# The last three stores of a decoder layer: a 256-column piece by ScalarE, GpSimd and a second store queue, and the stores of the block before it in halves

## The chip, the cores and the metric

The kernel runs on one core of a Trainium2 chip. The metric is the device time of one execution in microseconds, as the median of several runs. A core has TensorE (PE, matmuls), VectorE (DVE), ScalarE (ACT), GpSimd (POOL) and SyncE (SP), which here issues transfers. The core's 16 DMA engines move the data of all queues.

## The reference, cut to what matters

The layer takes x of 512 tokens by 1024 channels through two attention branches and a gated MLP. Only its last line bears on the change:

```python
ffn_out = (jax.nn.silu(h_gate) * h_val) @ w_down
x = _layer_norm(DEEPNORM_ALPHA * x + (1.0 + gt2) * ffn_out, ln2_g, ln2_b)
```

The layer norm takes each token's mean mu and variance over its 1024 channels and gives (x - mu) * rs * g + b, with rs = 1 / sqrt(var + 1e-5). All data is 32-bit float.

## The kernel before, in words

**Tiling.** The 512 tokens are four blocks of 128 rows (one row to a partition), each held as two tiles of 512 columns, `r[i][0]` and `r[i][1]`. The down projection is a chain of matmuls that ends with blocks 2 and 3. Blocks 0 and 1 are finished earlier, in `first_rows` (line 1298). Blocks 2 and 3 are finished by the last loop of `layer_kernel` (line 1345). For `i == 0` (block 2) columns 512 to 1023 are one piece of 512. For `i == 1` (block 3) they are two pieces of 256, whose matmuls run one after the other, so that only the last 256 columns come after the last matmul.

**The end of a block.** `tail` (line 1239) is called with the block number, 2 or 3, as its own `i`. It calls `ln_stats` (line 899), in which VectorE and ScalarE make mu and rs from the statistics in `st`. Line 1245 then has VectorE take (v - mu) * g of each piece, and line 1249 has VectorE take v * rs + b. After each piece's line 1249, line 1250 stores it from `nc.sync`, that is, from SP's queue. Block 2 has two pieces of 512 columns (256 KB each). Block 3 has three, called A, B and C here: A is columns 0 to 511 (256 KB), B is columns 512 to 767 and C is columns 768 to 1023 (128 KB each). B is the "middle" piece of the change.

**What sets the order.** SP runs in the order of the program, since `manual_schedule` at line 55 names that engine; a transfer waits there for the data, and what is behind it waits too. The other engines' instructions are ordered by a scheduler within the limits of their dependences: VectorE runs the small steps of `ln_stats` between the pieces of line 1245. The dependences are kept by part of a tile. ScalarE has nothing after the square root of line 903 in block 3, and GpSimd has nothing after the stores of line 1308.

Of the kernel before, what the change touches and what calls it, by code (L numbers as in the profile page):

```python
# [11 lines left out]
AF = mybir.ActivationFunctionType  # L12
ALU = mybir.AluOpType
# [11 lines left out]
H = T // 2  # L25
# [26 lines left out]
def layer_kernel(ctx: ExitStack, tc: tile.TileContext, out, xT, x, c8, wa0, wa1, bcol, w1, wct, wv, bf,  # L52
# [3 lines left out]
    V, S, G, PE = nc.vector, nc.scalar, nc.gpsimd, nc.tensor  # L56
# [63 lines left out]
    s = V.tensor_tensor(sel, s3, ident[:, 64:72], ALU.add)  # L120
    def top_half(ap):
        return ap.bitcast(BF16).rearrange("p (c t) -> p c t", t=2)[:, :, 1]

    ctop = top_half(crow)
    with tc.issue_after(s.ins):
        s = V.tensor_tensor(crow[32:40], c8s, top_half(c8s), ALU.subtract)
# [772 lines left out]
    def ln_stats(st):  # L899
        mv = cons.tile([P, 8], F32, name=nm("mv"), tag="mv", bufs=2)  # L900
        V.bn_aggr(mv[:, 0:2], st)
        v, s, y, t = mv[:, 2:3], mv[:, 3:4], mv[:, 4:5], mv[:, 5:6]
        S.activation(s, mv[:, 1:2], AF.Sqrt, bias=epsc)
        V.tensor_scalar_add(v, mv[:, 1:2], EPS)
        V.reciprocal(y, s)
        V.scalar_tensor_tensor(t, y, y, v, ALU.mult, ALU.mult)
        V.scalar_tensor_tensor(y, t, -3.0, y, ALU.add, ALU.mult)
        return mv[:, 0:1], y
# [16 lines left out]
    lnr = []  # L925
# [245 lines left out]
    for n in range(2 * FT):  # L1171
# [34 lines left out]
        if n % 2 == 1:  # L1206
            g, v = hc
# [31 lines left out]
    def tail(i, st, pieces, eng, src):  # L1239
        tb = slice(i * P, (i + 1) * P)  # L1240
        mu, rs = ln_stats(st[:, 0 : len(pieces), :])
        for (e, c0, c1), ps in zip(pieces, src):
            c = slice(e * 512 + c0, e * 512 + c1)
            v = r[i][e][:, c0:c1]
            V.scalar_tensor_tensor(v, v if ps is None else ps, mu, lnr[0][:, c], ALU.subtract, ALU.mult)
        for e, c0, c1 in pieces:
            c = slice(e * 512 + c0, e * 512 + c1)
            v = r[i][e][:, c0:c1]
            V.scalar_tensor_tensor(v, v, rs, lnr[1][:, c], ALU.mult, ALU.add)
            eng.dma_start(out[tb, c], v)  # L1250

    p1, u2, q1, u3, tm = [[fine(n) for _ in range(2)] for n in ("p1", "u2", "q1", "u3", "tm")]

# [63 lines left out]
    lnr = lnr2  # L1317
# [21 lines left out]
    s = V.tensor_tensor(r[3][1], r[3][1], W1[1], ALU.add)  # L1339
# [5 lines left out]
    for i in range(2):  # L1345
        pieces = [(1, 0, 512)] if i == 0 else [(1, 0, 256), (1, 256, 512)]
        for n, (e, c0, c1) in enumerate(pieces):
            ps = bank()[:, 0 : c1 - c0] if i else W1[0]
            for m in range(2 * n):
                PE.matmul(ps, idr, rest[:, m * 256 : m * 256 + 256], start=m == 0, stop=False)  # L1350
            for q in range(LATE):
                t = ops[FP - LATE + q][3]
                product(ps, t[:, top[i]], t[:, bot[i]], wc[q][0][:, c0:c1], wc[q][1][:, c0:c1], i == 1 and n == 0 and q == 0, q == LATE - 1, i == 0)
            v = r[2 + i][e][:, c0:c1]
            if n == 0:
                V.tensor_tensor(v, v, ps, ALU.add)
            V.bn_stats(sts[i][:, n + 1, :], ps if n else v)
        tail(2 + i, sts[i], [(0, 0, 512)] + pieces, nc.sync, [None, None, ps] if i else [None] * 2)
# [69 lines left out]
```

## Time and profile before

| what | value |
|---|---|
| median of 3 runs | 734.93 us (734.62 to 735.27) |
| the profiled execution, its time | 734.07 us |
| the profiled execution, its span | 732.3 us |
| PE busy in the span | 722.5 us (99%) |
| DVE, ACT, POOL busy | 601.1, 391.7, 88.0 us |

The span runs from the first to the last profiled instruction; 1.8 us of the profiled execution's time lie around it. Times in the rows are microseconds from the start of the span. A view of instructions has their start, their duration and the line of the kernel. A view of stretches has, for each, its length, each engine's busy time, the granted TensorE clock as a share of full speed, the mean busy share of the 16 DMA engines and the GB/s that they moved.

### The profile page before, as it was taken

The page shows a single profiled execution, that of the slowest core. Times are in us where ns is not written, and L with a number is a line of the kernel's source. Part 1 is how long each engine was busy: PE and PEld are TensorE (multiplying, and loading weights), DVE is VectorE, ACT ScalarE, POOL GpSimd, SP SyncE. Part 2 cuts the span into 40 slices and gives each one's busy share as a digit, 9 for nine tenths or more (in the row PEclk, how much of TensorE's full clock was granted, in tenths as well). Part 3 has the DMA queues.
Part 4 walks back from the last instruction along what each step waited for, and adds up shares of the span by engine and source line. Part 5 has one row for each costly group of instructions (what it writes and reads, how often), then busy time and mean ns, then how long its engine had stood idle before and what let it go on. Part 6 is the DMA issues. An engine that isn't in the chain of part 4 may idle for free.

```text
span 732.3 us, 9843 instructions
## 1 busy us (share of the span) xinstructions
PE 722.5 (99%) x3444; PEld 602.5 (82%) x3444; DVE 601.1 (82%) x1041; ACT 391.7 (53%) x684; POOL 88.0 (12%) x142
## 2 busy tenths in 40 slices
PE   8999999999999999999999999999999999999995
PEld 5878888888888888888889888888888888888885
DVE  7978799778898886883687999978887887679996
ACT  5576466686885754442056553454453544347550
POOL 1045224352010000000000001000011010000010
PEclk9999999999999999999999999999999999999998
DMA  9953435323332241632075688587698777657734
GB/s 358 404 207 126 173 116 197 148 88 115 118 116 99 75 171 59 224 128 86 1 259 139 216 248 238 169 252 227 189 359 245 217 238 209 200 164 224 219 91 93
DMA packets 45202, 131.96 MB, mean 180 GB/s; under 512 B 6136, under 2 KB 6656, under 8 KB 45152
## 3 DMA queue, kind: packets, MB, share of 16 engines
q1 hardware_dynamic: 37888, 112.61, 44.6%
q0 software_dynamic: 4224, 10.30, 7.4%
q10 hardware_dynamic: 3040, 8.42, 3.1%
q8 instruction: 27, 0.44, 0.2%
q14 instruction: 23, 0.19, 0.1%
HBM read 118.39 MB, written 12.85 MB: 179 GB/s over the span
## 4 chain that ended last, share of the span: by engine, by line
PE 97%; DVE 1%; DMA 0%; ACT 0%; issue 0%; DVEq 0%
PE ps L152 19%; PE ps L154 19%; PE ps L153 19%; PE ps L1148 5%; PE ps L1149 5%; PE ps L1150 5%; PE ps L369 5%; PE ps L613 3%; PE ps L595 2%; PE ps L521 2%; PE ps L523 2%; PE ps L522 2%; PE ps L939 2%; PE ps L941 2%; PE ps L940 2%; PE ps L547 1%
## 5 line engine op out<-in xcount | busy, mean ns | idle before, releaser
L217 ACT ACTIVATE wh<-raw 128x1024 fp32r<-128x1024 f32 (+1 forms) x105 | 109.0, 1040 | 106.5 <-PE ps L153 43.2
L94 DVE TENSOR_TENSOR wl<-raw,wh 128x1024 fp32r<-128x1024 f32 (+2 forms) x114 | 137.3, 1205 | 32.4 <-ACT wh L217 31.6
L152 PE MATMUL ps<-u2h,wh 128*128 128x512 f32 (+1 forms) x376 | 141.5, 376 | 0.0
L153 PE MATMUL ps<-u2l,wh 128*128 128x512 f32 (+1 forms) x376 | 141.3, 376 | 0.0
L154 PE MATMUL ps<-u2h,wl 128*128 128x512 f32 (+1 forms) x376 | 141.3, 376 | 0.0
L154 PEld LDWEIGHTS ps<-u2h,wl 128*128 128x128 f32 x376 | 70.8, 188 | 12.9
L152 PEld LDWEIGHTS ps<-u2h,wh 128*128 128x128 f32 x376 | 70.8, 188 | 12.7
L153 PEld LDWEIGHTS ps<-u2l,wh 128*128 128x128 f32 x376 | 70.8, 188 | 12.6
L152 PE MATMUL ps<-uh,wh 128*128 128x512 f32 x200 | 79.6, 398 | 0.0
L154 PE MATMUL ps<-uh,wl 128*128 128x512 f32 x200 | 78.2, 391 | 0.0
L153 PE MATMUL ps<-ul,wh 128*128 128x512 f32 x200 | 78.0, 390 | 0.0
L1201 ACT ACTIVATE cv<-ps,cw 128x512 f32<-128x512 f32 x44 | 34.0, 773 | 42.4 <-PE ps L154 36.0
L1202 DVE SCALAR_TENSOR_TENSOR cv<-ps,cw,cv 128x511 f32<-128x511 f32 x44 | 32.8, 746 | 21.6 <-ACT cv L1201 21.5
L154 PEld LDWEIGHTS ps<-uh,wl 128*128 128x128 f32 x200 | 37.6, 188 | 8.4
L153 PEld LDWEIGHTS ps<-ul,wh 128*128 128x128 f32 x200 | 37.7, 188 | 7.4
L152 PEld LDWEIGHTS ps<-uh,wh 128*128 128x128 f32 x200 | 37.6, 188 | 7.3
L240 DVE SCALAR_TENSOR_TENSOR raw<-raw,cbc 128x1024 f32<-128x1024 f32 x32 | 39.6, 1240 | 0.0
L575 POOL TENSOR_TENSOR pt<-pt,om 128x127 f32<-128x127 f32 (+3 forms) x32 | 38.6, 1217 | 1.3 <-DVE om L574 1.3
L181 POOL DMA_DIRECT2D raw<-in_wdp x10 | 8.9, 889 | 243.8 <-DMA raw<-in_wdp 227.7
L1203 DVE SCALAR_TENSOR_TENSOR cv<-ps,cw,cv 128x510 f32<-128x510 f32 x44 | 32.7, 744 | 0.4
L1209 ACT ACTIVATE cv<-cv 128x512 f32<-128x512 f32 x22 | 13.9, 631 | 34.1 <-DVE cv L1203 34.1
L574 DVE TENSOR_TENSOR_SCAN om<-om,dg 128x127 f32<-128x127 f32 (+3 forms) x32 | 28.8, 960 | 3.9 <-ACT om L569 3.9
(245 smaller groups left out, 1551.0 us busy)
## 6 DMA issues: line engine op xcount, KB each, us to landing
raw<-in_wup SPq DMA_DIRECT2D x44, 512.0 KB, 5.0
raw<-in_wa SPq DMA_DIRECT2D x32, 512.0 KB, 3.7
raw<-in_wct SPq DMA_DIRECT2D x25, 512.0 KB, 4.5
raw<-in_wdp SPq DMA_DIRECT2D x20, 512.0 KB, 5.3
wa<-in_wa SPq DMA_DIRECT2D x16, 512.0 KB, 8.7
raw<-in_wdp SPq DMA_DIRECT2D x22, 256.0 KB, 4.9
raw<-t SPq DMA_DIRECT2D x22, 256.0 KB, 4.3
raw<-in_wdp POOLq DMA_DIRECT2D x10, 512.0 KB, 7.7
```

What stands on the lines that cost most here:

```text
L94: state["read"] = V.tensor_tensor(o, i, fl(hi), ALU.subtract)
L152: PE.matmul(ps, wh, ah, start=first, stop=False)
L153: PE.matmul(ps, wh, al, start=False, stop=False)
L154: return PE.matmul(ps, wl, ah, start=False, stop=last)
L217: state["hi"] = S.activation(h[:, 0:cols], r[:, 0:cols], AF.Copy)
L240: state["read"] = V.scalar_tensor_tensor(wt[:, c], wt[:, c], 1.0, cbc[:, c] if by is None else by, ALU.mult, ALU.mult, accum_out=o)
L369: m = PE.matmul(grp[g], w, u, start=j == 0 and n == 0, stop=j == KT - 1 and n == 2)
L575: G.tensor_tensor(pt[b][:, s : e - 1], pt[b][:, s : e - 1], om[:, s + 1 : e], ALU.mult)
L1148: PE.matmul(ps, ah, bh, start=first, stop=False, skip_group_check=onto)
L1149: PE.matmul(ps, ah, bl, start=False, stop=False, skip_group_check=onto)
L1150: return PE.matmul(ps, al, bh, start=False, stop=last, skip_group_check=onto)
L1201: S.activation(t, ps, AF.Identity, bias=cw[:, n, 3:4], scale=cw[:, n, 2:3])
```

## The change

In `tail`, for the one piece whose block has three pieces and that starts at column 512 (piece B of block 3), line 1249 and the store of line 1250 are replaced by three instructions: ScalarE multiplies by rs, GpSimd adds b, and the store is issued from ScalarE's queue. In addition each store of block 2 becomes two stores of 256 columns (`H` is 256), both from SP's queue; A and C of block 3 are stored as before.

```diff
         for e, c0, c1 in pieces:
             c = slice(e * 512 + c0, e * 512 + c1)
             v = r[i][e][:, c0:c1]
+            if len(pieces) == 3 and c0 == 0 and e == 1:
+                S.activation(v, v, AF.Copy, scale=rs)
+                G.tensor_tensor(v, v, lnr[1][:, c], ALU.add)
+                S.dma_start(out[tb, c], v)
+                continue
             V.scalar_tensor_tensor(v, v, rs, lnr[1][:, c], ALU.mult, ALU.add)
-            eng.dma_start(out[tb, c], v)
+            for q in range(2) if i == 2 else [None]:
+                s = slice(0, c1 - c0) if q is None else slice(q * H, q * H + H)
+                eng.dma_start(out[tb, e * 512 + c0 : e * 512 + c1][:, s], v[:, s])
```

## Rows read from the trace of the kernel before

**Rows 1.** The page: span and the chain that ended last, by engine.

```profile
span 732.3 us, 9843 instructions
PE 97%; DVE 1%; DMA 0%; ACT 0%; issue 0%; DVEq 0%
```

**Rows 2.** Timeline of VectorE after the last matmul: start, duration, line, operation.

```profile
727.41 0.15 DVE L907 SCALAR_TENSOR_TENSOR mv<-mv 128x1 f32<-128x1 f32 x1
727.59 0.75 DVE L1249 SCALAR_TENSOR_TENSOR xn<-xn,mv,ln 128x512 f32<-128x512 f32 x1
...
728.26 0.88 DVE L1249 SCALAR_TENSOR_TENSOR xn<-xn,mv,ln 128x256 f32<-128x256 f32 x2
...
728.66 0.48 DVE L1249 SCALAR_TENSOR_TENSOR xn<-xn,mv,ln 128x256 f32<-128x256 f32 x1
```

**Rows 3.** Timeline of SP's queue: block 2's two stores merged, then A, B, C.

```profile
723.81 1.00 SPq L1250 DMA_DIRECT2D out<-xn  x2
...
728.37 0.33 SPq L1250 DMA_DIRECT2D out<-xn  x1
...
728.81 0.37 SPq L1250 DMA_DIRECT2D out<-xn  x1
...
729.28 0.39 SPq L1250 DMA_DIRECT2D out<-xn  x1
```

**Rows 4.** Stretches from block 2's first data to C's last.

```profile
724.60:726.10 1.50, 0.32 (x3) 0.12 (x1) 1.07 (x4) 0.29 (x1) 0.00 (x0) 1.00 0.92 350
726.10:727.60 1.50, 0.00 (x0) 0.00 (x0) 1.47 (x7) 0.00 (x0) 0.00 (x0) 1.00 0.01 5
727.60:729.20 1.60, 0.00 (x0) 0.00 (x0) 1.54 (x3) 0.00 (x0) 0.00 (x0) 0.77 0.00 0
729.20:729.90 0.70, 0.00 (x0) 0.00 (x0) 0.00 (x0) 0.00 (x0) 0.00 (x0) 0.50 0.96 367
729.90:730.30 0.40, 0.00 (x0) 0.00 (x0) 0.00 (x0) 0.00 (x0) 0.00 (x0) 0.50 0.99 336
730.30:730.70 0.40, 0.00 (x0) 0.00 (x0) 0.00 (x0) 0.00 (x0) 0.00 (x0) 0.50 0.92 320
```

**Rows 5.** DMA issues from 728.3 us on: count, KB each, median us to landing.

```profile
out<-xn SPq DMA_DIRECT2D x1, 256.0 KB, 2.0
out<-xn SPq DMA_DIRECT2D x2, 128.0 KB, 2.1
```

**Rows 6.** Line 1424, the program's end: SP's waits, ns min/median/max, first and last start.

```profile
L1424 SPq EVENT_SEMAPHORE  x12: 17/28/28, 729.7 to 732.2; - x12
```

**Rows 7.** ScalarE's groups over the whole span: busy us, mean ns, idle before.

```profile
L91 ACT ACTIVATE wdh<-rl 128x512 fp32r<-128x512 f32 x8 | 4.9, 617 | 0.3 <-DMA rl<-wgt 0.3
...
L91 ACT ACTIVATE hv<-sg 128x256 fp32r<-128x256 f32 x33 | 11.4, 405 | 0.0
```

**Rows 8.** Line 1307, ScalarE's scaling by rs: ns min/median/max, first and last start.

```profile
L1307 ACT ACTIVATE xn<-xn,mv x4: 705/708/727, 708.7 to 712.6; 128x512 f32<-128x512 f32 x4
```

**Rows 9.** Timeline, attention: GpSimd's 255-column product beside VectorE's scan, and later alone.

```profile
55.72 1.81 DVE L574 TENSOR_TENSOR_SCAN om<-om,dg 128x511 f32<-128x511 f32 x1
...
56.45 1.51 POOL L575 TENSOR_TENSOR pt<-pt,om 128x255 f32<-128x255 f32 x1
...
166.32 0.64 POOL L575 TENSOR_TENSOR pt<-pt,om 128x255 f32<-128x255 f32 x1
```

**Rows 10.** Line 1198, two stores to the output from ScalarE's queue: ns each, starts.

```profile
L1198 ACTq DMA_DIRECT2D out<-ln x2: 357/359/361, 535.2 to 536.6; - x2
```

**Rows 11.** DMA issues of ScalarE's queue: count, KB each, median us to landing.

```profile
t<-raw ACTq DMA_DIRECT2D x10, 512.0 KB, 2.7
...
out<-ln ACTq DMA_DIRECT2D x2, 512.0 KB, 5.8
```

**Rows 12.** The stretch in which line 1198 issues.

```profile
534.00:537.00 3.00, 3.00 (x15) 2.48 (x14) 1.08 (x4) 1.46 (x2) 2.08 (x4) 1.00 1.02 417
```

## Prediction, made before the run

> **What bounds the kernel now.** I read the page first, for what share of the span the change can touch at all. Its chain is 97% matmuls [rows 1], and the change touches none of them. It can act only after the last matmul, so I went to VectorE's timeline there: rs of block 3 is ready at 727.41 + 0.15 = 727.56 [rows 2]. From there to the end of the span are 732.3 - 727.56 = 4.74 us, 0.64% of the time. That is all the change has to work on.
>
> The next question is which wait ends last inside those 4.74 us. VectorE works through A, B and C back to back: A 727.59 to 728.34, B from 728.26, C from 728.66 to 729.14 [rows 2]. SP issues each store behind it, at 728.37, 728.81 and 729.28 [rows 3]. Read alone, those two views say that the chain is vector work and issue, and that taking B out of both would bring the end nearer. The table of stretches says otherwise. No data moves until 729.20, which is 0.83 us after A's issue. Then the DMA engines are 0.92 to 0.99 busy without a break until 730.70 [rows 4]. They move A (262,144 bytes) at 367 GB/s, 0.71 us, to 729.91, and B and C (131,072 bytes each) at 336 and 320 GB/s, 0.39 and 0.41 us, to 730.30 and 730.71. C was issued at 729.28, so by the same 0.83 us its data could have started at 730.11. The engines were not free for it until 730.30. **C has 0.19 us of slack**: it waits for transfers ahead of it, not for VectorE or SP. What follows is completion: the stores land 2.0 to 2.1 us after their issue, C at about 731.3 [rows 5], and SP's closing waits run to 732.2 [rows 6].
>
> So three things bound the end: the moment A is issued, 512 KB at some 350 GB/s, and the completion of the last piece. The change alters none of the three.
>
> **The change, part by part.**
>
> *B leaves VectorE.* That removes one line 1249 of 256 columns, 0.40 us of VectorE's path (728.26 to 728.66, start to start [rows 2]). C could then be done 0.40 us earlier, at 728.74, and be issued at 728.81, where B's store was. A stays first and starts at 727.59 as before; its store stays at 728.37.
>
> *B on ScalarE.* Line 1307 is this very operation at 512 columns, also behind a square root on ScalarE: 0.71 us, and no load of a function table stands among its instructions [rows 8], so I add none. Plain copies of 512 and 256 columns differ by 617 - 405 = 212 ns [rows 7], so I take 0.71 - 0.21 = 0.50 us. The handover from VectorE to SP takes 0.03 us (728.34 to 728.37 [rows 2, 3]); with the same to ScalarE it runs from 727.59 to 728.09.
>
> *B on GpSimd.* The nearest row is the 255-column product in attention: 0.64 us by itself, 1.51 us beside a scan on VectorE [rows 9]. With under 0.1 us of handover the add can start at 728.15, while A is still on VectorE until 728.34, with C next. Bounds: it ends at 728.79 if undisturbed and at 729.66 at the longer price. I take a wait for A and then the 0.64: 728.98. It is nearer the lower end because only 0.2 us of A is left when the add starts, against 1.08 us of the scan in the row of 1.51 (56.45 to 57.53). What VectorE loses in return is C: between nothing and the add's 0.64, so C ends between 728.74 and 729.38.
>
> By the Trainium skill, "SBUF — State Buffer", section "Who interferes with whom", a VectorE instruction with two SBUF inputs and a GpSimd one that reads SBUF exclude each other, and the later one waits for all of the other; this speaks against the change. By that rule the add would run from 728.34 to 728.98 and C from there to 729.46, and the data would end within 0.02 us of before. The trace agrees with the rule only in part: the product beside the scan would have ended at 57.53 + 0.64 = 58.17 by it, and ended at 57.96 [rows 9].
>
> *B's store from ScalarE's queue.* It issues at about 729.0 (729.7 at the longer price) and takes 0.36 us on that queue [rows 10]; nothing is behind it there. GpSimd too has nothing behind the add. First data by the same 0.83 us is at 729.83 (730.53). C's data can be ready by 728.81 + 0.83 = 729.64, or by 729.41 + 0.83 = 730.24 if the add holds C to 729.38. In the likely case both halves are there before or close to when A's data is through at 729.91, in one order or the other, and the third piece is needed only at 730.30, that is, issued by 729.47. So both moves cost or gain **nothing**: the cover is A's 0.71 us and one half's 0.39 us on the DMA engines. If that cover were gone, the gain would be the earlier issue of the last store, at most 729.28 - 728.81 = 0.47 us. At the longer price for the add, B's data starts at 730.53 instead of 730.30: 0.23 us later.
>
> *Block 2's stores in halves.* SP issues four instead of two: two behind the first instruction of line 1249, from 723.81, and two behind the second. Before, the two took until 724.81 [rows 3]. Stores of block 3 follow each other at 0.44 to 0.47 us, so the extra pair adds 0.9 us at most and SP is done by 725.8, or 2.6 us before A needs it at 728.37. The halves move at about 330 instead of 350 to 367 GB/s, 0.1 us more for 512 KB, so that the engines finish near 726.3; they then stand idle until 729.20 [rows 4]. Cost zero; cover 2.6 us on SP and 2.9 us on the DMA engines, and 0.9 us if that were gone.
>
> *The closing.* SP has 12 waits of up to 28 ns here [rows 6], and a different last store or a second queue can shift a few. I take -0.1 to +0.1 us.
>
> **Sum.** Against the profiled execution (734.07 us, span 732.3 us): 0 for vector work and issue, 0 for block 2, about -0.1 for a last store that no longer queues behind two others on SP, hence some 734.0 for such an execution. It was 0.86 us under the median of 734.93, so I put the change on the median: 734.8 us.
>
> **The rivals.**
>
> *Issue-bound after all (faster, 0.04).* If the engines' 0.92 to 0.99 busy share hides a wait for C's issue, the last store comes 0.47 us sooner: 734.5. For it: 320 GB/s in the last stretch is below A's 367. Against: no gap of idle engines between 729.20 and 730.70 [rows 4].
>
> *GpSimd and VectorE in each other's way (0.05).* The add at 1.51 us makes B the last piece, +0.23 us: 735.2. For: the 1.51 us of the nearest row [rows 9]. Against: only 0.2 us of A remain when the add is ready.
>
> *ScalarE's queue is slow to deliver (slower, 0.03).* Its two earlier stores to the output took 5.8 us from issue to landing [rows 11], against 2.0 to 2.1 on SP's queue [rows 5]. With B issued at 729.0 and landing 5.8 us later, at 734.8 against 731.3 now, the end comes 3.5 us later: 738.4. It costs something once the landing takes longer than 2.3 us, and can be measured from 3.8 us on. Against: those were 512 KB each, at DMA engines that were full (share 1.02 [rows 12]); ten other stores of 512 KB from that queue landed in 2.7 us [rows 11], of which 512 KB at 350 GB/s are 1.5.
>
> *The change does not reach B.* The condition holds for exactly one piece: three pieces only in block 3, and column 512 only in B. I give it no chance.
>
> **How the numbers follow.** About 0.2%, 1.47 us, is what a measurement of this kernel can tell from no change. On the slow side only the slow queue exceeds it, 0.03, and 0.01 is left for what the rows do not show: 0.04. A gain of 1.47 us would be a third of the 4.74 us; no case here has it, and 0.02 is left for the unseen. The rest, 0.85 for the forecast and 0.09 for the two small rivals, is within: 0.94. The range takes the spread of the three runs (734.62 to 735.27), less 0.47 and 0.1 below, plus 0.23 and 0.1 above: 734.0 to 735.6.
>
> **What would show it.** Right: A issued 0.81 us after rs, the DMA engines full from its first data for 1.5 us without a gap, and some 3.1 us from that first data to the end of the span. ScalarE 0.50 us, GpSimd's add 0.64 to 0.9 us, C's end between 728.74 and 729.38 on this clock. Block 2's four stores done 2.5 us or more before A's. Wrong: idle DMA engines between the three pieces, a landing of B much over 2.1 us, or a span before the last matmul that is not the same to a few tenths.

## The result, and the profile after

The changed kernel takes 737.09 us in the median of 8 runs (736.48 to 737.71), against 734.85 us for the kernel before (8 runs, 734.62 to 735.27). The ratio is 1.0028, with a 95% interval of 1.0020 to 1.0037: it is slower by some 2 us, where the prediction said 734.8 us, at most 735.6, and gave a slowdown one chance in 25.

The span of the profiled execution grew from 732.3 to 734.7 us. Not all of these 2.4 us belong to the change: rs of block 3 is there at 727.73 + 0.15 = 727.88 instead of 727.56, so 0.32 us were lost before the first changed instruction that matters, among matmuls that are the same in both programs. Such differences come and go between executions (in experiment 11, whose program is that of before up to this point, rs is there at 728.50); what stands behind rs is the subject here, and the times below are given from rs.

The stages of the last block come first. The four fences are the timelines of VectorE, ScalarE, GpSimd and SP after the change (start, duration, line, operation); line 1254 is the old 1249, and 1250 to 1252 are the three new instructions.

```profile
727.73 0.15 DVE L907 SCALAR_TENSOR_TENSOR mv<-mv 128x1 f32<-128x1 f32 x1
727.92 1.61 DVE L1254 SCALAR_TENSOR_TENSOR xn<-xn,mv,ln 128x512 f32<-128x512 f32 x2
```

```profile
727.92 0.51 ACT L1250 ACTIVATE xn<-xn,mv 128x256 f32<-128x256 f32 x1 [1.54 <-DVE mv L907]
729.28 0.34 ACTq L1252 DMA_DIRECT2D out<-xn  x1
```

```profile
728.51 0.74 POOL L1251 TENSOR_TENSOR xn<-xn,ln 128x256 f32<-128x256 f32 x1 [13.52 <-ACT xn L1250]
```

```profile
728.70 0.33 SPq L1257 DMA_DIRECT2D out<-xn  x1
...
729.56 0.33 SPq L1257 DMA_DIRECT2D out<-xn  x1
```

Everything here is as forecast. ScalarE needs 0.51 us (0.50 forecast), GpSimd's add ends at 729.25, which is rs + 1.37 (1.42 forecast), and C is ready at 729.53, which is rs + 1.65 (between 1.18 and 1.82 forecast). A is issued 0.82 us after rs, as before. The stretches show the engines full from the first data to the last, over the same 1.5 to 1.6 us as in [rows 4] (columns as there):

```profile
727.10:729.50 2.40, 0.00 (x0) 0.00 (x0) 2.36 (x6) 0.51 (x1) 0.74 (x1) 0.97 0.01 2
729.50:730.20 0.70, 0.00 (x0) 0.00 (x0) 0.03 (x1) 0.00 (x0) 0.00 (x0) 0.50 0.94 357
730.20:730.60 0.40, 0.00 (x0) 0.00 (x0) 0.00 (x0) 0.00 (x0) 0.00 (x0) 0.50 0.96 330
730.60:731.10 0.50, 0.00 (x0) 0.00 (x0) 0.00 (x0) 0.00 (x0) 0.00 (x0) 0.50 0.82 285
731.10:734.70 3.60, 0.00 (x0) 0.00 (x0) 0.00 (x0) 0.00 (x0) 0.00 (x0) 0.50 0.00 0
```

The data of all three stores is out at 731.1. Before, it was out at 730.7, with rs 0.32 us earlier, so that the stores are level within 0.1 us. But then 3.6 us pass to the end of the span, where 1.6 passed before. The loss lies behind the last byte. What happens there is the program's closing, and all of it has one line, 1431 (1424 before). On each engine's own queue (POOLq is GpSimd's, SPq is SP's) it has DRAIN instructions and the semaphores at which all engines meet. The view of that line, in the changed kernel (count, ns min/median/max, first and last start):

```profile
L1431 SPq EVENT_SEMAPHORE  x11: 17/28/28, 729.9 to 734.6; - x11
L1431 POOLq EVENT_SEMAPHORE  x4: 17/17/17, 734.0 to 734.6; - x4
L1431 POOLq DRAIN  x3: 46/98/5447, 728.5 to 734.4; - x3
L1431 SPq DRAIN  x3: 7/7/7, 731.7 to 734.2; - x3
```

And the same view of the kernel before, from which [rows 6] has only SP's waits:

```profile
L1424 POOLq EVENT_SEMAPHORE  x4: 17/17/17, 731.6 to 732.2; - x4
L1424 POOLq DRAIN  x3: 46/98/8165, 713.5 to 732.0; - x3
L1424 SPq DRAIN  x3: 7/7/7, 731.5 to 731.8; - x3
```

SP's own first DRAIN, behind its waits for the stores, stands at 731.7 (731.5 before). GpSimd's first semaphore of the closing stands at 734.0, against 731.6 before. Between them lies GpSimd's longest DRAIN: it starts with the add at 728.5 and lasts 5.447 us, to 733.9. Before, it lasted even longer, 8.165 us, but it started at 713.5 with GpSimd's last store and was over by 721.7, ten microseconds before anyone asked. SP's drains take 7 ns in both kernels, though SP issues transfers too. The other engines show the wait, under a misleading name. SP's waits in the changed kernel:

```profile
SPq L1431 <- PEq L1431: 2.9, 2, 2.4
SPq L1431 <- DMA out<-xn: 1.2, 3, 0.5
```

and in the kernel before:

```profile
SPq L1424 <- DMA out<-xn: 1.2, 3, 0.5
SPq L1424 <- PEq L1424: 0.7, 2, 0.5
```

The wait for the stores is the same 1.2 us. The wait at the meeting of the engines grew from 0.7 to 2.9 us. The view puts it down to PE, whose queue has been idle for long; it is a meeting of all engines, and GpSimd comes last.

### The profile page after: what moved, and what is told of

Read it like the earlier page. It is cut to its first block, busy times and chain, and to the rows that moved or that the text cites. A ratio compares the mean times of both kernels' runs of the same rounds, so it can differ in the third digit from the quotient of the medians.

```text
span 734.7 us, 9844 instructions
## 1 busy us (share of the span) xinstructions
PE 723.1 (98%) x3444; PEld 602.2 (82%) x3444; DVE 600.5 (82%) x1040; ACT 392.2 (53%) x685; POOL 88.6 (12%) x143
## 4 chain that ended last, share of the span: by engine, by line
PE 97%; DVE 1%; DMA 0%; ACT 0%; DVEq 0%; issue 0%
PE ps L152 19%; PE ps L154 19%; PE ps L153 19%; PE ps L1148 5%; PE ps L1150 5%; PE ps L1149 5%; PE ps L369 5%; PE ps L613 3%; PE ps L595 2%; PE ps L521 2%; PE ps L523 2%; PE ps L522 2%; PE ps L939 2%; PE ps L940 2%; PE ps L941 2%; PE ps L547 1%
```

## The experiments

**Theory D**: GpSimd's closing drain outlasts its last instruction by some 4.7 us, and every engine waits for it. **Rival Q**: ScalarE's queue or the halves of block 2 deliver late. **Rival C**: VectorE and GpSimd block each other. Four kernels take these apart.

**1. B's add on VectorE.**

```diff
                 S.activation(v, v, AF.Copy, scale=rs)
-                G.tensor_tensor(v, v, lnr[1][:, c], ALU.add)
+                V.tensor_tensor(v, v, lnr[1][:, c], ALU.add)
                 S.dma_start(out[tb, c], v)
```

> The changed kernel with one word altered: B's add of b runs on VectorE instead of GpSimd; ScalarE's scaling, the store from ScalarE's queue and block 2's halves stay. Theory D (GpSimd's closing drain at the program's end lasts some 4.7 us beyond its last instruction, and every engine waits for it): GpSimd's last work is line 1315's stores at about 715 again, its drain is over by about 722, and the time is that of before within 0.3 us, 734.6 to 735.1, that is 2.0 to 2.4 us under the changed kernel. Rival Q (ScalarE's queue delivers late, or the halves cost): still about 737. Rival C (VectorE and GpSimd block each other): part of it comes back, since B's add returns to VectorE, 735 to 736.

Measured: 734.71 us, 0.9999 of the kernel before (0.9990 to 1.0008). The whole loss goes with the one instruction; ScalarE's scaling, its queue and the halves stay and cost nothing that can be told.

**2. A GpSimd copy of one column, late, in the kernel before.**

```diff
             eng.dma_start(out[tb, c], v)
+        if len(pieces) == 3:
+            G.tensor_copy(const([P, 1], F32, "touch"), v[:, 0:1])
```

> The kernel before, with one GpSimd copy of 128x1 added that reads C's result after VectorE's last instruction and that nothing reads. No other part of the change is in it. Theory D: the copy is done at about 729.3, the drain at about 729.3 + 4.7 = 734.0 instead of being over long before 731.6, and the time is 2.0 to 2.6 us over before, 736.9 to 737.5. Rival Q: no store differs, so 734.9. Rival C: nothing of VectorE runs beside it, so 734.9.

Measured: 736.73 us, 1.0027 (1.0016 to 1.0037). None of the change is in this kernel but a GpSimd instruction of 0.19 us on data that nobody needs, and it costs what the change costs. Its timeline and its closing:

```profile
729.34 0.19 POOL L1252 COPY touch<-xn 128x1 f32<-128x1 f32 x1 [14.54 <-DVE xn L1249]
```

```profile
L1426 POOLq DRAIN  x3: 46/93/4871, 729.3 to 734.7; - x3
```

**3. The same copy, early.**

```diff
             eng.dma_start(out[tb, c], v)
+        if len(pieces) == 2:
+            G.tensor_copy(const([P, 1], F32, "touch"), v[:, 0:1])
```

> The same GpSimd copy of 128x1, but reading block 2's last result, at about 724.5. Theory D: the drain is over at about 724.6 + 4.7 = 729.3, before the last store has landed at 731.3, and costs nothing: 734.6 to 735.1. If instead any GpSimd instruction behind the stores of line 1308 lengthens the end, whenever it runs: about 737, as in the late one.

Measured: 734.51 us, 0.9997 (0.9988 to 1.0006). The drain is as long as in 2, but it starts at 725.2 and is over by 730.1, before the last store has landed:

```profile
L1426 POOLq DRAIN  x3: 46/97/4871, 725.2 to 732.7; - x3
```

So it is not the instruction that costs, but how late it stands. SP was through with the stores at 731.5 in the kernel before; a GpSimd instruction is free there if it ends by about 731.5 - 4.7 = 726.8, which is before rs exists (727.56).

**4. Only the halves of block 2.**

```diff
-            eng.dma_start(out[tb, c], v)
+            for q in range(2) if i == 2 else [None]:
+                s = slice(0, c1 - c0) if q is None else slice(q * H, q * H + H)
+                eng.dma_start(out[tb, e * 512 + c0 : e * 512 + c1][:, s], v[:, s])
```

> The kernel before with block 2's stores in halves and nothing else of the change. Theory D and the prediction on record: no change, 734.6 to 735.1, at most 0.1 us less because the last store's wait stands last in SP's closing list. Rival Q in the form that the halves cost: up to 737.

Measured: 734.64 us, 0.9999 (0.9990 to 1.0008): nothing, as forecast. Theory D stands, Q and C fall.

**What the 4.7 us are.** The drain at the program's start took 0.18 us, over four memsets; that at the end takes 4.7 us more than the instruction under it. Two kernels ask whether transfers that GpSimd issues are behind this.

**5. GpSimd's transfers to other queues.** Left on GpSimd are the first gate rows, four transfers of line 652 and one of line 654: five, not the two of the expectation below. The sums of lines 181 and 1315 are left out.

```diff
-                G.dma_start(it[3], it[5], accum_op=ALU.add)
+                pass
-        G.dma_start(s2t[n][66:68, :], chi[h : h + 1, :, :])
-        G.dma_start(m2t[n][64:66, :], chi[h : h + 1, :, :])
+        S.dma_start(fl(s2t[n][66:68, :]), fl(chi[h : h + 1, :, :]))
+        S.dma_start(fl(m2t[n][64:66, :]), fl(chi[h : h + 1, :, :]))
-                G.dma_start(d, t)
+                S.dma_start(d, t)
-            G.dma_start(dst, r)
+            S.dma_start(dst, r)
-                rows = gate_rows(1 + n // 30, G)
+                rows = gate_rows(1 + n // 30, S)
-            G.dma_start(out[tb, c], v, accum_op=ALU.add)
+            nc.sync.dma_start(out[tb, c], v)
```

> The changed kernel with all but two of GpSimd's transfers given to other queues (line 181's accumulating load and line 1315's accumulation onto the output are left out, so the sums that they make are missing); GpSimd's add for B stays its last work. It asks what the 4.67 us of the closing drain belong to. If they come with any GpSimd compute instruction at the end: the drain again ends 4.6 to 4.7 us after the add, whatever was transferred. If they come from transfers that GpSimd issued late in the program: the drain is over within 0.1 us of the add, as the drain at the program's start is within 0.1 us of a memset.

**6. Only the four stores of line 1315 away from GpSimd.**

```diff
-            G.dma_start(out[tb, c], v, accum_op=ALU.add)
+            nc.sync.dma_start(out[tb, c], v)
```

> The changed kernel with only the four last GpSimd transfers (blocks 0 and 1, line 1315) given to SP as plain stores, which leaves out their addition onto the output. All earlier GpSimd transfers stay. If the drain waits for recent transfers: shorter than the 4.67 us after the add. If it does not: 4.6 to 4.7 us after the add, and the time stays near 737.

Measured: 737.12 us for 5 and 737.99 us for 6 (one run each). In both rs is later than in the changed kernel (730.41 and 729.42 against 727.88); why was not looked into. The drains of the two, 5 and then 6:

```profile
L1431 POOLq DRAIN  x3: 40/102/1547, 731.0 to 735.1; - x3
...
L1251 POOL TENSOR_TENSOR xn<-xn,ln x1: 1009/1009/1009, 731.0 to 731.0; 128x256 f32<-128x256 f32 x1
```

```profile
L1431 POOLq DRAIN  x3: 46/93/5389, 730.0 to 735.9; - x3
...
L1251 POOL TENSOR_TENSOR xn<-xn,ln x1: 1011/1011/1011, 730.1 to 730.1; 128x256 f32<-128x256 f32 x1
```

Less the add beneath it, the drain is 0.54 us in 5 and 4.38 us in 6. That fits neither of the two answers that the expectation offered: no recent transfer is left in 6, and yet nearly all of it stays. What fits is a count. The program has 56 transfers issued by GpSimd (its issues in the DMA view sum to that), 52 in 6 and 5 in 5; four fewer shorten the drain by 0.33 us, 51 fewer by 4.17 us, 0.082 us each both times. From this **theory N**, 0.09 us and 0.082 us for each transfer issued so far, counted from the end of the add, forecast three more kernels (7 to 9); 10 was added after the time of 9.

**7. 40 transfers.** Of the edits of 5, only that of lines 443 and 444:

```diff
-        G.dma_start(s2t[n][66:68, :], chi[h : h + 1, :, :])
-        G.dma_start(m2t[n][64:66, :], chi[h : h + 1, :, :])
+        S.dma_start(fl(s2t[n][66:68, :]), fl(chi[h : h + 1, :, :]))
+        S.dma_start(fl(m2t[n][64:66, :]), fl(chi[h : h + 1, :, :]))
```

> The changed kernel with the 16 small transfers of the decay rows (lines 443 and 444, in attention, at about 160 us) issued by ScalarE instead of GpSimd; the result is the same. GpSimd then issues 40 transfers in the whole program instead of 56. So far the drain lasted beyond the add 4.67 us with 56, 4.34 with 52 and 0.50 with 5. Theory N (it is 0.09 us and 0.082 us for each transfer that GpSimd has issued since the start, however long ago): 0.09 + 40 x 0.082 = 3.4 us, and the time is 1.3 us under the changed kernel, 735.6 to 736.0. Rival K (a constant of some 4.5 us once GpSimd has issued enough or large transfers): 4.6 to 4.7 us, and 737.

**8. 72 transfers.** Sixteen transfers of 8 bytes are added. Their code stands behind attention, but the scheduler had them issued at the program's start, from 1.4 to 13.0 us, and not after attention as the expectation says:

```diff
     G.memset(epsc, EPS)
+    more = const([1, 32], F32, "more")
+    for q in range(16):
+        G.dma_start(more[:, 2 * q : 2 * q + 2], lnrow[0:1, 2 * q : 2 * q + 2])
```

> The changed kernel with 16 transfers of 8 bytes added on GpSimd after attention, into a tile that nothing reads: 72 transfers instead of 56. Theory N: 0.09 + 72 x 0.082 = 6.0 us of drain beyond the add, and 1.3 us more than the changed kernel, 738.2 to 738.6. Rival K: 4.6 to 4.7 us, and 737. If the bytes count and not the number: 4.7 us too.

**9. 21 transfers.** The edit of 7, and from those of 5:

```diff
-                G.dma_start(d, t)
+                S.dma_start(d, t)
-            G.dma_start(dst, r)
+            S.dma_start(dst, r)
-                rows = gate_rows(1 + n // 30, G)
+                rows = gate_rows(1 + n // 30, S)
```

> A version of the change that keeps GpSimd's add and gives the same result: of GpSimd's 56 transfers all those that neither accumulate nor belong to the first gate row go out from ScalarE's queue, which leaves 21. Theory N: 0.09 + 21 x 0.082 = 1.8 us, so that GpSimd is through at about 731.1, before SP's closing waits at 731.5, and the change costs nothing: 734.4 to 735.1. Rival K: 737.

**10. 30 transfers.** The edit of 7, and from those of 5:

```diff
-                rows = gate_rows(1 + n // 30, G)
+                rows = gate_rows(1 + n // 30, S)
```

> The version with 21 transfers had its drain over before the last store, as theory N says, and still took 735.9 us in the median, with runs from 735.0 to 737.9. This one moves only the 16 decay rows and ten of the gate rows to ScalarE's queue and leaves lines 1019 and 1024 (the prepared weights, which later loads read) on GpSimd: 30 transfers. Theory N: 0.09 + 30 x 0.082 = 2.55 us beyond the add, so GpSimd is through some 0.1 us after SP, and the end costs 0.1 to 0.3 us. If lines 1019 and 1024 on ScalarE's queue made the other version uneven: 734.8 to 735.4, without runs over 736.5. If moving the small transfers did: uneven again, about 736.

The drains of 7, 8, 9 and 10:

```profile
L1431 POOLq DRAIN  x3: 46/98/4137, 729.6 to 734.6; - x3
```

```profile
L1434 POOLq DRAIN  x3: 46/99/6756, 728.9 to 736.2; - x3
```

```profile
L1431 POOLq DRAIN  x3: 46/98/2591, 729.0 to 733.1; - x3
```

```profile
L1431 POOLq DRAIN  x3: 46/102/3324, 732.1 to 736.2; - x3
```

With the add's own time taken off (1.009 and 1.011 us in 5 and 6, 0.740 to 0.744 us in the others), against a line drawn through the two outermost, 5 and 72:

| GpSimd's transfers | kernel | drain less add, us | 0.130 + 0.0817 x count |
|---|---|---|---|
| 5 | experiment 5 | 0.538 | 0.539 |
| 21 | experiment 9 | 1.847 | 1.846 |
| 30 | experiment 10 | 2.580 | 2.581 |
| 40 | experiment 7 | 3.396 | 3.398 |
| 52 | experiment 6 | 4.378 | 4.378 |
| 56 | the change | 4.707 | 4.705 |
| 72 | experiment 8 | 6.013 | 6.012 |

The five in the middle lie within 3 ns of the line. The 16 transfers of 8 bytes added in 8, in the first 13 us, count as much, each, as the four of 256 KB taken away in 6, the last before the end; so do those of attention taken away in 7 (160 to 215 us in the changed kernel). Theory N holds, rival K falls.

The time follows in 8, and in 7 nearly. Experiment 7 took 736.26 us, 1.0017 (1.0008 to 1.0026): 0.26 us above the 735.6 to 736.0 that was expected, which its interval, 735.5 to 736.8 us at a median of 734.92 before, takes in. Experiment 8 took 738.29 us, 1.0046 (1.0033 to 1.0059), as expected.

Experiments 9 and 10 had their drains as forecast, in 9 over at 731.6 while SP's closing waits were still going on, and were slow all the same: 735.91 us, 1.0016 (1.0006 to 1.0026), with runs from 734.98 to 737.93, against 734.4 to 735.1 expected, and 736.12 us, 1.0023 (1.0012 to 1.0033). In their profiled executions the end itself is as theory N has it. Rs and SP's first DRAIN, in 9 and then in 10:

```profile
728.31 0.15 DVE L907 SCALAR_TENSOR_TENSOR mv<-mv 128x1 f32<-128x1 f32 x1
...
L1431 SPq DRAIN  x3: 7/7/7, 732.5 to 732.9; - x3
```

```profile
731.33 0.15 DVE L907 SCALAR_TENSOR_TENSOR mv<-mv 128x1 f32<-128x1 f32 x1
...
L1431 SPq DRAIN  x3: 7/7/7, 735.6 to 735.9; - x3
```

The same readings for all; rs is in us from the start of the span, the rest in us after rs:

| kernel | rs | GpSimd's long drain over | SP's first DRAIN | end of the span |
|---|---|---|---|---|
| before | 727.56 | before rs | 3.9 | 4.7 |
| the change | 727.88 | 6.0 | 3.8 | 6.8 |
| experiment 5 | 730.41 | 2.1 | 4.1 | 4.9 |
| experiment 6 | 729.42 | 6.0 | 4.3 | 6.8 |
| experiment 7 | 729.07 | 4.7 | 3.7 | 5.8 |
| experiment 8 | 728.30 | 7.3 | 3.8 | 8.1 |
| experiment 9 | 728.46 | 3.2 | 4.0 | 4.9 |
| experiment 10 | 731.48 | 3.9 | 4.1 | 5.0 |

The span ends 0.8 to 1.1 us behind whichever of the two is later. In these executions of 5, 9 and 10 that is SP, as before, and what makes them slower lies for the most part ahead of rs. In 10 a reason shows in the middle of the program. ScalarE's conversions there (groups in the stretch from 455 to 475 us: count, busy us, mean ns, idle before and what ended it):

```profile
L1201 ACT ACTIVATE cv<-ps,cw 128x512 f32<-128x512 f32 x4 | 3.1, 772 | 3.6 <-DMA grow<-growt 2.7 <-DVE wdl L94 0.8
```

In its order of instructions ScalarE comes to the gate row's broadcast, waits 2.7 us for the row to land, and the conversion behind it comes late. TensorE has 1.99 of 4.00 us busy from 464 to 468, where it had 4.00 before (10, then the kernel before; columns as in [rows 4]):

```profile
464.00:468.00 4.00, 1.99 (x10) 1.36 (x8) 4.00 (x7) 0.10 (x1) 0.00 (x0) 1.00 0.57 174
...
464.00:468.00 4.00, 4.00 (x19) 3.30 (x19) 3.54 (x6) 2.11 (x5) 0.00 (x0) 1.00 0.30 121
```

That is 2.0 of the 3.9 us by which rs is later than before; the rest was not followed up. So my reading that lines 1019 and 1024 made 9 uneven was wrong: 10 does not have them and is as uneven, and the gate rows are common to both. For 9 itself this was not shown; its profiled execution, one of its shorter ones (735.17 us), lacks that wait.

**11 and 12. The stores by themselves.** In 11 B goes out from ScalarE's queue and VectorE still makes it; in 12 block 3 is finished in four pieces of 256 columns, stored in turn by SP and ScalarE.

```diff
-            eng.dma_start(out[tb, c], v)
+            (S if len(pieces) == 3 and c0 == 0 and e == 1 else eng).dma_start(out[tb, c], v)
```

> The kernel before with one thing of the change: B's store goes out from ScalarE's queue, while VectorE still makes B. The prediction's step that C waits for the DMA engines and not for its issue: C's issue moves from 0.14 us to under 0.1 us behind its data, the last data comes within 0.1 us of before, and the time is 734.4 to 735.0, not to be told from before. Rival Q: landing of B over 2.3 us and a longer time, up to 738.

```diff
+        if i == 3:
+            pieces = [(e, c0, c0 + 256) for e in range(2) for c0 in (0, 256)]
-        for e, c0, c1 in pieces:
+        for n, (e, c0, c1) in enumerate(pieces):
...
-            eng.dma_start(out[tb, c], v)
+            (S if i == 3 and n % 2 else eng).dma_start(out[tb, c], v)
```

> A try at a version under both: the kernel before, with block 3's last step and stores in four pieces of 256 columns, issued in turn by SP and ScalarE. If the end is bound by the first data and then by the DMA engines, the first data comes some 0.35 us earlier (a 256-column instruction instead of 512) and the last some 0.1 to 0.3 us earlier, since VectorE needs 0.40 us for each piece and the engines 0.39: 734.3 to 734.8. If VectorE's fourth instruction and its issue bind instead: no gain, or 0.1 us lost.

Measured: 734.58 us, 1.0000 (0.9991 to 1.0009) and 734.71 us, 1.0003 (0.9994 to 1.0012). In 11, SP issues C at once:

```profile
728.53 1.54 DVE L1249 SCALAR_TENSOR_TENSOR xn<-xn,mv,ln 128x512 f32<-128x512 f32 x3
```

```profile
730.10 0.33 SPq L1250 DMA_DIRECT2D out<-xn  x1
```

C is ready at 730.07 and issued 0.03 us later, instead of 0.14 (729.14 to 729.28 [rows 2, 3]). Yet from rs (728.50 here) to the last data, at 731.7, are 3.2 us, as they were before (727.56 to 730.7). C did wait for the DMA engines. In 12 the first data came earlier, some 1.4 us after rs (728.25 to a little over 729.6) instead of 1.64:

```profile
729.50:729.60 0.10, 0.00 (x0) 0.00 (x0) 0.10 (x2) 0.00 (x0) 0.00 (x0) 0.50 0.00 0
729.60:731.20 1.60, 0.00 (x0) 0.00 (x0) 0.35 (x1) 0.00 (x0) 0.00 (x0) 0.50 0.92 315
```

But the last came not more than 0.1 us earlier, since VectorE's and the engines' 0.4 us for each piece follow. Neither kernel is faster than the kernel before.

## Why the prediction was wrong

The time lay outside the range and on the side that had 0.04. Step by step:

- **What bounds the end**: "the moment A is issued, 512 KB at some 350 GB/s, and the completion of the last piece" was right for the kernel before, and "The change alters none of the three" was right too. It was wrong as a full list. A fourth thing ends there, GpSimd's closing drain, which had ten microseconds to spare before and -2 us after.
- **B leaves VectorE, B on ScalarE**: right, to 0.01 us for ScalarE.
- **B on GpSimd**: the add itself was right (0.74 us, ending at rs + 1.37 against 1.42). VectorE's C took 0.94 instead of 0.48 us beside it, inside the bounds. By the Trainium skill, "SBUF — State Buffer", section "Who interferes with whom", C would have waited for all of the add from A's end on, to an estimated 728.67 + 0.64 + 0.48 = 729.79; it ended at 729.53, so the trace again agrees only in part. C and A in the changed kernel (busy us, mean ns):

```profile
L1254 DVE SCALAR_TENSOR_TENSOR xn<-xn,mv,ln 128x256 f32<-128x256 f32 x1 | 0.9, 944 | 0.0
L1254 DVE SCALAR_TENSOR_TENSOR xn<-xn,mv,ln 128x512 f32<-128x512 f32 x1 | 0.8, 750 | 0.0
```

- **The step that failed** is one clause in the part on B's store: "GpSimd too has nothing behind the add." Behind it stands the drain, 4.7 us with this program's 56 transfers, and the end of the program waits for it. The words on the kernel before, "GpSimd has nothing after the stores of line 1308", have the same gap: there the drain of 8.165 us follows. The view that shows it was in use: [rows 6] was taken from the view of line 1424, and two lines below it stands GpSimd's DRAIN of 8.165 us. I read SP's lines of that view, because SP came last, and did not ask what an engine whose last work moves from 714.7 to 729.2 brings along.
- **B's store from ScalarE's queue, and its rival**: B landed 1.9 us after its issue, not 5.8. The rival that ended on the slower side had the right sign for the wrong reason.
- **Block 2 in halves**: zero, as forecast (experiment 4).
- **The closing**: "-0.1 to +0.1 us" held for SP: its DRAIN came at rs + 3.8 (731.7) against rs + 3.9 before. It missed GpSimd.
- **The size**: GpSimd's first closing semaphore came at 734.0 - 727.88 = rs + 6.1, against 731.6 - 727.56 = rs + 4.0 before. These 2.1 us are the 0.0028 of 734.85 us that the runs show. Of the prediction's signs, "some 3.1 us from that first data to the end of the span" is the one that fails: it was 734.7 - 729.5 = 5.2.

## What to carry to other kernels

Before giving an idle engine work near the end of a program, read the closing instructions of that engine, not only what is queued behind the work: an engine with nothing to do may still have something to finish. On GpSimd, count the transfers that it issues in the whole program; here its last compute instruction had to end some 0.09 + 0.0817 us x that count before the other engines were through (4.7 us with 56), and longer before where the last instruction is itself a transfer. Having VectorE do the late work gave the loss back (experiment 1); moving transfers to ScalarE's queue shortened the drain but made the middle of the program slower in experiment 10. A wait at a meeting of all engines is put down to one of them; look for the engine whose own first closing instruction comes last.

## What the runs showed of the hardware that I had not expected

- GpSimd's drain at the end grows by 0.0817 us with each transfer that it has issued since the start, whatever its size (8 bytes or 256 KB) and whether it was issued in the first 13 us or at 710, on top of 0.13 us: 0.54 us for 5 to 6.01 us for 72. What the drain does with each was not seen and stays open.
- Behind a transfer instead of a compute instruction the drain was longer: 8.165 us with the last store's 1.11 us in it, so some 7.1 us beyond it, with the same 56 transfers. In the traces it follows the data of that store: the last packet of GpSimd's queue was through at 719.02, and the drain was over 2.68 us later, at 721.70. In experiments 1, 4, 11 and 12, which end GpSimd's work with the same store, the drain lasted 7.97 to 8.26 us and was over 2.68 to 2.69 us behind that queue's last packet each time.
- A GpSimd copy of 128 values, 0.19 us long and read by nobody, made the kernel 2 us slower (736.73 against 734.74 us).
